# The second FFN product of a one-core diffusion step by Strassen's algorithm

## The chip, the cores and the metric

The kernel runs on one core of a Trainium2 chip. A core has five engines with an instruction queue each: TensorE (matrix products, PE in the profile; its weight loads are PEld), VectorE (DVE), ScalarE (ACT), GpSimd (POOL) and SyncE (SP). SP only issues DMA transfers here, and a few stand on POOL. Results of matrix products go to PSUM; everything else lies in SBUF or in DRAM. The metric is the device time of one execution in microseconds (us).

## The reference, cut to what matters

One layer takes 1024 latent and 128 context tokens of 1024 features through a normalisation, a mixer (recurrence and Fourier branch) and an FFN, with shared weights. The part that the change touches is the FFN and the last normalisation:

```python
    h2 = rmsnorm(x, norm2_g) * (1.0 + scale2) + shift2
    uv = h2 @ ffn_w_in                     # first FFN product:  1024 x 5632
    u = uv[..., :D_FF]
    v = uv[..., D_FF:]                     # D_FF = 2816
    x = x + gate2 * ((jax.nn.silu(u) * v) @ ffn_w_out)   # second FFN product: 2816 x 1024
    ...
y_prompt = rmsnorm(xp, final_g)            # final normalisation, context tokens
y_sample = rmsnorm(xs, final_g)            # and latent tokens
```

All of it is float32.

## The kernel before

**Layout.** Features lie on the 128 partitions and the 1152 tokens (T) along the free axis: x is 8 tiles of 128x1152, and the hidden features silu(u)\*v are 22 tiles (NJ) of 128x1152. A float32 product is made in three passes: each operand is split into a high half (a rounding cast to fp32r by ScalarE) and a low half (the operand minus the high half, by VectorE), and high x high, high x low and low x high are added up in PSUM.

**First FFN product.** It is done by Strassen's algorithm already. A unit j (22 of them) pairs the 128 features j of u with the same ones of v, and the tokens are two halves of 576 (H). The seven products P1, P6, P2, P7, P5, P4, P3 of a unit take 24 matmuls of 128x288 each (`mm_half`, L943), so 168 in a unit; the weights of a product are 512 columns, cast by L1149 and subtracted by L1150 on VectorE, after the weight sums L1161 to L1168. Behind each product VectorE adds its result in (`e6`, `e7`, `e5`, `e4`, `e3`; L1218 to L1239). `e4` and `e3` end with the multiplication by silu(u), and POOL writes the two halves of the hidden tile j to DRAM (`s_d`, L1235 and L1243). The products P1 and P2 of the units 0 to 5 run ahead, beside the second normalisation.

**Second FFN product, as it was.** It is a plain product. `GRPS` cuts the 22 hidden tiles into a group of two and five of four. For a group, `fo_step` goes through the 8 feature blocks m: 3 passes of 3 chunks of 384 tokens for each hidden tile (`mm3`, L241), all in one PSUM tile; `post` adds it, times gate2, to the residual x2[m] on VectorE (L913, L921). The residual's tiles are fetched from DRAM in the first group (L1300). Beside a group the hidden tiles of the next one are fetched (`s_load`, L1261) and split (`s_split`, L245 and L246). The last group runs by token spans instead (`last_step`, L1333: tokens 640 to 1151, 0 to 383, 384 to 639) and adds up the squares of x2 for the final normalisation, partly on POOL. `stat_sum` turns those sums into factors (TensorE sums over the partitions, L260, ScalarE's square root, VectorE's reciprocal), `final_bcast` spreads the factors over the partitions with TensorE (L280, from diagonals of L279), and `final_out` (L1356) makes the outputs.

**What sets the order.** The kernel is scheduled by hand: the instructions of an engine run in the order in which the program emits them. The program is a list of steps; for each the main loop calls `before`, then `advance` (loads of weights on SP some pieces ahead, casts and low halves of the next pieces), then `pe` (the matmuls), `post` and `after`. What is emitted in a step's `post` therefore stands behind the weight splits for the steps ahead. `woven` is a list of tasks that go between the matmuls of a step. Tiles come from pools of fixed size, and an instruction that takes a buffer waits until its last reader is through: 33 buffers of 128x1152 for most operands (`TT`), 4 for short-lived ones such as the fetched hidden tiles `sld` (`LL`), and weight pools that are opened anew by `scope_w`: in the first product 4 raw tiles and 5 split ones, in the second 3 raw tiles of 1024 columns and 3 split ones. In PSUM `G` tiles hold 2 chunks of 288, `Z` tiles 3 chunks of 384.

**The handover.** The last unit's products do more than the others: after the matmuls of P2, `last_p2` fetches and splits the two hidden tiles of the first group, and after those of P3, `last_p3` opens the second product's weight pools and issues the first weight loads.

## Time and profile before

| | |
|---|---|
| Time, median of 3 runs | 1692.13 us (1679.47 to 1692.36) |
| Time of the profiled execution | 1690.14 us |
| Its span | 1688.3 us |
| Mean granted clock of TensorE | 0.994 |
| TensorE busy | 1643.7 us (97% of the span), 10680 matmuls |
| VectorE busy | 1027.6 us (61%) |
| ScalarE busy | 598.0 us (35%) |
| GpSimd busy | 113.8 us (7%) |
| First FFN product, unit by unit | up to 1394.3 us |
| Second FFN product | 1394.5 to 1677.1 us |
| Final normalisation behind it | 1677.1 to 1688.3 us |

Times in the trace count from the start of the span. A row of a timeline has the start, the duration in us, engine, line, operation and tiles (result <- operands); what stands in brackets is the idle time of the engine ahead of it and what ended it. "x10" behind shapes is the number of instructions in a row that the line stands for. Names are the program's, without buffer numbers: g and z are PSUM tiles, w the unit's work tiles, ho and hl split weights, wr raw weights. SPq is SP's DMA queue.

### The profile page before, as it was taken

Reading aid. Unit: us, or ns where it says so; the run is one execution under the profiler, and the core shown is the slowest. Engines: PE = TensorE matmul, PEld = TensorE weight load, DVE = VectorE, ACT = ScalarE, POOL = GpSimd, SP = SyncE. Lnnn points to the kernel's source line nnn. Section 1 sums busy time; section 2 is a strip of 40 time slices with the busy share of each in tenths; the row PEclk is TensorE's granted clock in tenths of the full one; section 3 lists DMA queues with packets and bytes.
Section 4 is the critical chain, followed back from the end, with each engine's and each line's share of the span. In section 5 each row is a group of like instructions: output and inputs, shape, how many; then the busy total and the mean of one; then the engine's idle time right before and its main releaser. Section 6 shows DMA issues by size and latency. Waiting matters only on the chain.

```text
span 1688.3 us, 25378 instructions
## 1 busy us (share of the span) xinstructions
PE 1643.7 (97%) x10680; PEld 1612.8 (96%) x10680; DVE 1027.6 (61%) x1454; ACT 598.0 (35%) x777; POOL 113.8 (7%) x153
## 2 busy tenths in 40 slices
PE   6899999999999999999999999999999999999997
PEld 3799999999999998899999899999999999999997
DVE  6678976777877235734368765555555556444446
ACT  6583127474664223412156322222222232111112
POOL 0200002010101000000000000000000000000012
PEclk9999999999999999999999999999999999999999
DMA  9028832222223035521533232222122236222203
GB/s 376 15 89 311 278 112 98 80 80 92 77 83 129 28 116 192 208 97 61 175 104 121 75 109 87 79 74 70 67 79 72 72 122 245 83 104 80 98 10 113
DMA packets 54177, 192.44 MB, mean 114 GB/s; under 512 B 6384, under 2 KB 8832, under 8 KB 54064
## 3 DMA queue, kind: packets, MB, share of 16 engines
q1 hardware_dynamic: 44624, 154.24, 26.7%
q0 software_dynamic: 9440, 36.58, 5.7%
q8 instruction: 84, 1.38, 0.3%
q14 instruction: 29, 0.24, 0.0%
HBM read 149.45 MB, written 41.30 MB: 113 GB/s over the span
## 4 chain that ended last, share of the span: by engine, by line
PE 77%; DVE 4%; issue 3%; ACT 1%; DMA 0%; POOL 0%; DVEq 0%; SPq 0%; ACTq 0%; POOLq 0%
PE z L241 35%; PE g L943 33%; PE z L1333 3%; PE g L818 1%; PE z L613 1%; PE z L614 1%; PE z L612 1%; PE a L686 1%; PE a L652 0%; DVE ho L1150 0%; DVE hl L207 0%; DVE plo L246 0%; POOL sq L536 0%; DMA sld<-s_d 0%; PE bc L280 0%
## 5 line engine op out<-in xcount | busy, mean ns | idle before, releaser
L241 PE MATMUL z<-hhi,hl 128*128 128x384 f32 x1344 | 280.8, 340 | 0.0
L241 PEld LDWEIGHTS z<-hhi,hl 128*128 128x128 f32 x1344 | 237.8, 188 | 0.8 <-issue 0.8
L943 PE MATMUL g<-b,ho 128*128 128x288 f32 x1584 | 218.9, 296 | 2.2 <-DVE ho L1150 1.2
L943 PEld LDWEIGHTS g<-b,ho 128*128 128x128 f32 x1584 | 213.8, 189 | 2.6 <-DVE ho L1150 1.5
L241 PE MATMUL z<-shi,hl 128*128 128x384 f32 x864 | 175.7, 338 | 0.6 <-DVE x L916 0.6
L206 ACT CAST hl<-wr 128x1024 fp32r<-128x1024 f32 x86 | 89.4, 1042 | 189.4 <-PE z L241 169.6
L241 PEld LDWEIGHTS z<-shi,hl 128*128 128x128 f32 x864 | 153.4, 188 | 1.2 <-issue 0.6
L241 PE MATMUL z<-hlo,hl 128*128 128x384 f32 x672 | 154.5, 338 | 0.0
L943 PE MATMUL g<-t,ho 128*128 128x288 f32 x1056 | 149.5, 297 | 2.8 <-DVE t L1089 2.8
L207 DVE TENSOR_TENSOR hl<-wr,hl 128x1024 fp32r<-128x1024 f32 x86 | 104.6, 1221 | 76.8 <-ACT hl L206 76.0
L943 PEld LDWEIGHTS g<-t,ho 128*128 128x128 f32 x1056 | 144.2, 190 | 3.2 <-DVE t L1089 3.1
L943 PE MATMUL g<-thi,ho 128*128 128x288 f32 x704 | 126.2, 296 | 0.0
L241 PEld LDWEIGHTS z<-hlo,hl 128*128 128x128 f32 x672 | 120.9, 188 | 0.0
L1149 ACT CAST ho<-wr 128x512 fp32r<-128x512 f32 x110 | 64.8, 618 | 155.3 <-DVE wr L1163 139.0
L1150 DVE TENSOR_TENSOR ho<-wr,ho 128x512 fp32r<-128x512 f32 x110 | 75.4, 687 | 60.8 <-ACT ho L1149 60.7
L921 DVE SCALAR_TENSOR_TENSOR x<-z,mods,x 128x768 f32<-128x768 f32 x40 | 40.7, 1017 | 112.6 <-PE z L241 112.6
L943 PEld LDWEIGHTS g<-thi,ho 128*128 128x128 f32 x704 | 104.7, 189 | 0.0
L943 PE MATMUL g<-mx,hl 128*128 128x288 f32 x768 | 102.1, 294 | 0.0
L943 PEld LDWEIGHTS g<-mx,hl 128*128 128x128 f32 x768 | 101.6, 188 | 0.0
L241 PE MATMUL z<-slo,hl 128*128 128x384 f32 x432 | 99.2, 338 | 0.0
L420 DVE SCALAR_TENSOR_TENSOR junk<-adar,cb 128x1024 f32<-128x1024 f32 x64 | 78.3, 1224 | 4.8 <-DMA adar<-in_ada_dram 2.9
L241 PE MATMUL z<-xchi,hl 128*128 128x384 f32 x384 | 79.5, 338 | 0.6 <-ACT sg L391 0.6
(258 smaller groups left out, 2643.4 us busy)
## 6 DMA issues: line engine op xcount, KB each, us to landing
wr<-in_w_uv_dram SPq DMA_DIRECT2D x50, 512.0 KB, 3.6
wr<-in_w_in_dram SPq DMA_DIRECT2D x32, 512.0 KB, 4.2
adar<-in_ada_dram SPq DMA_DIRECT2D x32, 512.0 KB, 5.6
s_d<-w POOLq DMA_DIRECT2D x44, 288.0 KB, 2.4
sld<-s_d SPq DMA_DIRECT2D x22, 576.0 KB, 4.7
wr<-in_w_ff_dram SPq DMA_DIRECT2D x22, 512.0 KB, 3.7
ada<-in_ada_dram SPq DMA_DIRECT2D x16, 512.0 KB, 10.5
wr<-in_w_out_dram SPq DMA_DIRECT2D x13, 512.0 KB, 4.2
```

The costliest lines, as they stand in the source:

```text
L206: nc_a.copy(h[:, 0], r)
L207: nc_v.tensor_sub(h[:, 1], r, h[:, 0].bitcast(F32))
L241: nc_t.matmul(ps[:, c, :CH], w, xx[:, c * CH:(c + 1) * CH], start=(k == first and i == 0), stop=(k == last and i == 2))
L420: nc_v.scalar_tensor_tensor(env["j"], w, 1.0, env["c"][v], op0=ALU.mult, op1=ALU.mult, accum_out=out[:, v:v + 1])
L612: nc_t.matmul(ps, th, rh, start=(k == 0), stop=False)
L613: nc_t.matmul(ps, th, rl, start=False, stop=False)
L614: nc_t.matmul(ps, tl, rh, start=False, stop=(k == KD - 1))
L921: nc_v.scalar_tensor_tensor(dst[:, :768].rearrange("p (c n) -> p c n", c=2), ps[:, 0:2, :CH], mods[:, gq, 0, m:m + 1], src[:, :768].rearra ...
L943: nc_t.matmul(ps[:, c, :HC], w(e, k), xx[:, c * HC:(c + 1) * HC], start=(first and i == 0 and j == 0), stop=(last and i == len(ks) - 1 and ...
L1149: nc_a.copy(h[:, 0], src)
L1150: low = lambda: nc_v.tensor_sub(h[:, 1], src, h[:, 0].bitcast(F32))
L1333: nc_t.matmul(ps[:, b, :hi - lo], ww, xx[:, lo:hi], start=(j == js[0] and i == 0), stop=(j == js[-1] and i == 2))
```

## The change

The second product is now done by Strassen's algorithm too. The 22 hidden tiles are taken as 11 pairs (even tile 2q and odd tile 2q+1), the 8 feature blocks as 4 pairs, the tokens as two halves of 576. B11 and B21 are the first half's tokens of the even and the odd tiles, B12 and B22 the second half's. Operand sums: T1 = B12 - B11, T3 = B22 - B12, T2 = B22 - T1, T4 = B21 - T2. The four weight sums are made in the same manner from the four quarters of the weights.

- `e4` writes a unit's first half to DRAM as B11 or B21. `e3` of an even unit makes T1 and writes it; `e3` of an odd unit writes B22 and makes and writes T3, T2 and T4. B12 isn't written. DRAM holds seven operands (`op_d`) of 11 blocks of 576 tokens in place of `s_d`.
- `ws_tasks` makes the weight sums in 11 parts, one in each of the units 8 to 18: `load` (after P1: four loads of 512 columns on SP), `sums` (after P4: five VectorE operations of 512 columns, and four writes by POOL to `ws_d`).
- The second product takes the products in the order P1, P6, P2, P7, P5, P4, P3 and for each the four feature pairs (`f_steps`). A step pair has 11 blocks, 3 passes and 2 chunks of 288 with `mm_half` in a G tile, the weights being one load of 1408 columns (`fr`), split in two parts of 768 and 640 columns (`f_items`). `f_post` adds the seven results in and updates x2; the sums of squares are on VectorE alone. `after` fetches and splits the next product's operand during the current one, two blocks at a time.
- At the handover `last_p2` fetches and splits the first three parts of B11, and `last_p4` the other three.
- P3 comes last. The final normalisation of the first token half runs woven into it (`fin_sum`, `fin_bcast`, `fin_out`); the last feature pair (`f_last`) goes through its first 288 tokens for all 11 blocks and then through the other 288, and the tail has 3 token tiles left.

The diff's core:

```diff
...
-GRPS = [[0, 1]] + [list(range(s, s + 4)) for s in range(2, NJ, 4)]
+NK = NJ // 2
+WB = NK * P
...
+        open_pool("w", *[[("wraw0", 3), ("whl0", 3)], [("wraw1", 4), ("who1", 5)], [("fraw2", 3), ("fop2", 3)]][n])
...
-    s_d = dr.tile([NJ, P, T], F32, name="s_d")
+    op_d = dr.tile([7, P, NK * H], F32, name="op_d")
+    ws_d = dr.tile([4, P, 4 * WB], F32, name="ws_d")
...
             nc_v.tensor_mul(un.w1[:, H:T], un.w1[:, H:T], un.w2[:, 0:H])
-            nc_p.dma_start(s_d[j][:, 0:H], un.w1[:, H:T])
+            nc_p.dma_start(op_dram("B21" if j % 2 else "B11", j // 2), un.w1[:, H:T])
...
             nc_v.tensor_mul(un.w2[:, H:T], un.w2[:, H:T], un.w1[:, 0:H])
-            nc_p.dma_start(s_d[j][:, H:T], un.w2[:, H:T])
+
+            s1_, s2_, q = un.w1[:, H:T], un.w2[:, H:T], j // 2
+            if j % 2 == 0:
+                nc_v.tensor_sub(un.w1[:, 0:H], s2_, s1_)
+                nc_p.dma_start(op_dram("T1", q), un.w1[:, 0:H])
+                even["w"] = (un.w1, un.w2)
+            else:
+                v1, v2 = even.pop("w")
+                nc_p.dma_start(op_dram("B22", q), s2_)
+                nc_v.tensor_sub(v2[:, 0:H], s2_, v2[:, H:T])
+                nc_p.dma_start(op_dram("T3", q), v2[:, 0:H])
+                nc_v.tensor_sub(v2[:, H:T], s2_, v1[:, 0:H])
+                nc_p.dma_start(op_dram("T2", q), v2[:, H:T])
+                nc_v.tensor_sub(un.w1[:, 0:H], s1_, v2[:, H:T])
+                nc_p.dma_start(op_dram("T4", q), un.w1[:, 0:H])
...
+        def load():
+            box["t"] = []
+            for a in (((0, 0), (1, 0)), ((1, 1), (0, 1))):
+                t = TT("ws", shape=(P, 2, 512))
+                for i, (r, q) in enumerate(a):
+                    nc_s.dma_start(t[:, i], w_ff[r, q][:, o])
+                box["t"].append(t)
+
+        def sums():
+            t, u = box.pop("t")
+            nc_v.tensor_add(u[:, 0], u[:, 0], t[:, 1])
+            nc_v.tensor_add(u[:, 1], u[:, 1], t[:, 0])
+            nc_v.tensor_sub(t[:, 1], t[:, 0], t[:, 1])
+            nc_v.tensor_sub(t[:, 0], u[:, 0], t[:, 0])
+            nc_v.tensor_sub(u[:, 1], u[:, 1], u[:, 0])
+            for i, q in enumerate((u[:, 0], t[:, 0], t[:, 1], u[:, 1])):
+                nc_p.dma_start(ws_d[i][:, o], q)
...
+    def op_load(name, g):
         t = LL("sld")
...
+        n = 2 if g < NK // 2 else 1
+        nc_s.dma_start(t[:, :n * H], op_dram(name, 2 * g, n))
...
+    FSEQ = (("P1", (0, 0), "B11"), ("P6", 1, "T2"), ("P2", (0, 1), "B21"), ("P7", 2, "T3"), ("P5", 0, "T1"),
+            ("P4", (1, 1), "T4"), ("P3", 3, "B22"))
...
+        def dma():
+            r = box["r"] = pools["fraw"].tile([P, WB], F32, name="fr", tag="fr")
+            a = w_ff[src[0], src[1]] if isinstance(src, tuple) else ws_d[src]
+            nc_s.dma_start(r[:], a[:, fp * WB:(fp + 1) * WB])
+
+        def prep(k0, k1):
+            h = pools["fop"].tile([P, 2, KA * P], F32R, name="fo", tag="fo")
+            n, q = (k1 - k0) * P, box["r"][:, k0 * P:k1 * P]
+            nc_a.copy(h[:, 0, :n], q)
+            nc_v.tensor_sub(h[:, 1, :n], q, h[:, 0, :n].bitcast(F32))
...
+    def f_post(name, fp, ps):
...
+        if name == "P1":
+            nc_a.copy(two(v0), z)
+        elif name == "P6":
+            nc_v.tensor_add(two(v1), z, two(v0))
...
+        elif name == "P4":
+            nc_v.tensor_add(two(v0), z, two(v0))
+            add_x(m2, 0, v0)
+            del VV[fp]
+            for m in (m1, m2):
+                acc_sq(m, 0, H)
...
+        def after(h):
+            if pi == 0:
+                x2[h] = TT(f"x2_{h}")
+                nc_s.dma_start(x2[h][:], x2_d[h])
...
+            if 1 <= h <= 4:
+                op_split(nxt, h - 1)
+            if h < 6:
+                op_load(nxt, h)
...
+            for c in range(2):
+                for k in range(NK):
+                    if c == 1 and k == 7:
+                        fin_sum(CH1[0])
+                    if c == 1 and k == 10:
+                        fin_bcast(CH1[0])
...
-                for q in GRPS[0]:
-                    s_load(q)
-                    s_split(q)
+                for g in range(3):
+                    op_load("B11", g)
+                    op_split("B11", g)
...
+                for g in range(3, 6):
+                    op_load("B11", g)
+                    op_split("B11", g)
...
+    for j in range(8, 8 + NK):
+        load, sums = ws_tasks(j - 8)
+        us = unit_last[j]
+        us["P1"].after, us["P4"].after = load, sums
...
+                if fp == 0:
+                    steps[-2].before = lambda: woven.extend([[], [], [], [], [lambda: fin_sum(HALF0)], []])
+                    steps[-1].before = lambda: woven.extend([[], [lambda: fin_bcast(HALF0)], [], [], []])
...
+    c0, c1 = CH1
+    fin_out(c0, [(0, 1), (2, 3)])
+    fin_sum(c1)
+    fin_out(c0, [(4, 5)])
+    fin_bcast(c1)
+    fin_out(c0, [(6, 7)])
+    fin_out(c1, [(0, 1), (2, 3), (4, 5), (6,), (7,)])
```

Where instructions stand now, at three places.

VectorE in one of the units 8 to 18 of the first product, behind its fifth product; w are the work tiles of units, ws the raw tiles of weight sums, ho split weights, g PSUM. Before:

```order
L1232 TENSOR_TENSOR w_11399<-g,w_11311 128x576
L1234 TENSOR_TENSOR w_11311<-w_11311,w_11399 128x576
L1150 TENSOR_TENSOR ho<-wr,ho 128x512
L1239 TENSOR_TENSOR w_11311<-g,w_11311 128x576
L1242 TENSOR_TENSOR w_11399<-w_11399,w_11311 128x576
L1150 TENSOR_TENSOR ho<-sx,ho 128x512 x2
L1218 TENSOR_TENSOR w_11527<-g,w_11527 128x576
```

And now, from the weight sums on, which stand behind the two operations of `e4`:

```order
L1295 TENSOR_TENSOR ws<-ws 128x512
L1296 TENSOR_TENSOR ws<-ws 128x512
L1297 TENSOR_TENSOR ws<-ws 128x512
L1298 TENSOR_TENSOR ws<-ws 128x512
L1299 TENSOR_TENSOR ws<-ws 128x512
L1156 TENSOR_TENSOR ho<-wr,ho 128x512
L1245 TENSOR_TENSOR w_11504<-g,w_11504 128x576
L1248 TENSOR_TENSOR w_11598<-w_11598,w_11504 128x576
L1258 TENSOR_TENSOR w_11366<-w_11598,w_11366 128x576
L1260 TENSOR_TENSOR w_11366<-w_11598,w_11272 128x576
L1262 TENSOR_TENSOR w_11504<-w_11504,w_11366 128x576
L1156 TENSOR_TENSOR ho<-sx,ho 128x512 x2
```

Five weight sums stand between `e4` and the next low half of weights, and in an odd unit three operand sums between `e3` and the two after it (in an even unit one).

SP at the handover; wr and fr are raw weights, sld fetched operands, x_0 to x_7 the residual. Before:

```order
L1145 DMA wr<-in_w_uv_dram 128x1024
L1261 DMA sld<-s_d 128x1152 x2
L1300 DMA x_0_12326<-x_d 128x1152
L195 DMA wr<-in_w_ff_dram 128x1024 x2
L1300 DMA x_1_12371<-x_d 128x1152
L195 DMA wr<-in_w_ff_dram 128x1024 x3
L1261 DMA sld<-s_d 128x1152
```

And now:

```order
L1151 DMA wr<-in_w_uv_dram 128x1024
L1311 DMA sld<-op_d 128x1152 x5
L1311 DMA sld<-op_d 128x576
L1338 DMA fr<-in_w_ff_dram 128x1408 x3
L1436 DMA x_0_12680<-x_d 128x1152
L1311 DMA sld<-op_d 128x1152
L1436 DMA x_1_12719<-x_d 128x1152
```

Six operand loads stand ahead of the second product's first weights, where two and a load of the residual stood before; the weights' loads have 1408 columns instead of 1024.

VectorE from the last sum of squares on; x_0 to x_7 are the residual, yt the outputs, bc the spread factors, dg the diagonals. Before:

```order
L934 TENSOR_TENSOR acc_14112<-acc_14112,sq_14534 128x256
L1356 SCALAR_TENSOR_TENSOR yt<-x_4_12467,vec,bc 128x384
L1356 SCALAR_TENSOR_TENSOR yt<-x_5_12495,vec,bc 128x384
L267 RECIPROCAL rr<-r 128x4
L279 TENSOR_SCALAR dg<-ident,rr 128x128 x2
L1356 SCALAR_TENSOR_TENSOR yt<-x_6_12526,vec,bc 128x384
L1356 SCALAR_TENSOR_TENSOR yt<-x_7_12554,vec,bc 128x384
```

And now:

```order
L1376 TENSOR_TENSOR acc_14460<-acc_14460,sq_15140 128x288
L1477 SCALAR_TENSOR_TENSOR yt<-x_0_12680,vec,bc 128x288
L1477 SCALAR_TENSOR_TENSOR yt<-x_1_12719,vec,bc 128x288
L1477 SCALAR_TENSOR_TENSOR yt<-x_2_12769,vec,bc 128x288
L1477 SCALAR_TENSOR_TENSOR yt<-x_3_12812,vec,bc 128x288
L269 RECIPROCAL rr<-r 128x6
L1477 SCALAR_TENSOR_TENSOR yt<-x_4_12862,vec,bc 128x288
L1477 SCALAR_TENSOR_TENSOR yt<-x_5_12905,vec,bc 128x288
L281 TENSOR_SCALAR dg<-ident,rr 128x128 x2
L1477 SCALAR_TENSOR_TENSOR yt<-x_6_12951,vec,bc 128x288
L1477 SCALAR_TENSOR_TENSOR yt<-x_7_12992,vec,bc 128x288
```

Four outputs of the 288 tokens before the last stand ahead of the reciprocal, two ahead of the diagonals and two behind them; eight outputs of the last 288 tokens follow, as eight of 256 tokens did before.

## Rows read from the trace of the kernel before

**Rows 1.** The page: engines' busy time (share of the span, instructions), the chain's shares, weight loads.

```profile
PE 1643.7 (97%) x10680; PEld 1612.8 (96%) x10680; DVE 1027.6 (61%) x1454; ACT 598.0 (35%) x777; POOL 113.8 (7%) x153
...
PE 77%; DVE 4%; issue 3%; ACT 1%; DMA 0%; POOL 0%; DVEq 0%; SPq 0%; ACTq 0%; POOLq 0%
...
wr<-in_w_uv_dram SPq DMA_DIRECT2D x50, 512.0 KB, 3.6
```

**Rows 2.** Busy by stretch: us, PE, PEld, DVE, ACT, POOL (instructions), clock, DMA share, GB/s.

```profile
941.00:1000.00 59.00, 56.12 (x407) 55.64 (x407) 42.28 (x64) 14.75 (x25) 3.24 (x6) 0.97 0.32 102
1000.00:1100.00 100.00, 100.00 (x752) 100.00 (x751) 58.12 (x86) 23.00 (x41) 5.39 (x10) 1.00 0.25 83
1394.30:1420.00 25.70, 25.13 (x143) 24.45 (x142) 20.25 (x29) 8.16 (x8) 0.54 (x1) 1.00 0.93 357
1623.00:1677.20 54.20, 54.06 (x318) 49.62 (x316) 29.18 (x58) 16.31 (x29) 17.93 (x18) 1.00 0.12 42
1677.20:1688.30 11.10, 1.77 (x8) 1.45 (x8) 7.60 (x19) 1.07 (x3) 0.36 (x1) 0.64 0.66 224
```

**Rows 3.** The chain that ended last, in order of time: start, us, what.

```profile
853.02 1.26 PE bc L280 x10
...
895.65 1.01 PE st L260 x10
...
949.85 444.80 PE g L943 x3322
...
1408.09 215.17 PE z L241 x1224
...
1673.52 0.67 PE bc L280 x6
```

**Rows 4.** Timeline of VectorE, 1140 to 1165 us.

```profile
1141.87 0.76 DVE L1228 TENSOR_TENSOR w<-g,w 128x576 f32<-128x576 f32 x1 [1.84 <-PE g L943]
1142.55 0.68 DVE L1161 TENSOR_TENSOR sx<-wr 128x512 f32<-128x512 f32 x1
...
1164.27 0.76 DVE L1228 TENSOR_TENSOR w<-g,w 128x576 f32<-128x576 f32 x1 [1.84 <-PE g L943]
```

**Rows 5.** DMA of 1394 to 1420 us: totals; issues with KB each and median us to landing.

```profile
DMA packets 2313, 9.17 MB, mean 353 GB/s; under 512 B 269, under 2 KB 269, under 8 KB 2311
...
sld<-s_d SPq DMA_DIRECT2D x5, 576.0 KB, 8.6
```

**Rows 6.** The tile s_d: from its writes' issue to landing.

```profile
DMA to landing us min/median/max: 2.4/2.4/8.8
```

**Rows 7.** Timeline of SP and TensorE, 1380 to 1412 us.

```profile
1384.63 0.81 SPq L195 DMA_DIRECT2D wr<-in_w_ff_dram  x2
...
1394.47 0.68 PE L241 MATMUL z<-shi,hl 128*128 128x384 f32 x3
```

**Rows 8.** Stretches of 1 us, columns as in rows 2.

```profile
950.00:951.00 1.00, 1.00 (x5) 1.00 (x6) 0.41 (x1) 1.00 (x3) 0.00 (x0) 0.50 0.00 0
...
952.00:953.00 1.00, 1.00 (x6) 1.00 (x5) 0.23 (x1) 0.00 (x0) 0.00 (x0) 0.50 0.00 0
```

**Rows 9.** Timeline of TensorE, 944.9 to 957 us.

```profile
949.85 2.88 PE L943 MATMUL g<-t,ho 128*128 128x288 f32 x10 [2.83 <-DVE t L1089]
```

**Rows 10.** Timeline of all engines, 1672 to 1689 us.

```profile
1680.76 4.49 DVE L1356 SCALAR_TENSOR_TENSOR yt<-x,vec,bc 128x384 f32<-128x384 f32 x10
1680.79 1.20 PE L280 MATMUL bc<-dg,ones 128*128 128x128 f32 x4 [0.98 <-DVE dg L279]
```

**Rows 11.** Groups by line and form, 1394 to 1689 us: busy us, mean ns, idle before.

```profile
L246 DVE TENSOR_TENSOR slo<-sld,shi 128x1152 fp32r<-128x1152 f32 x20 | 27.0, 1349 | 3.1 <-ACT shi L245 3.1
L207 DVE TENSOR_TENSOR hl<-wr,hl 128x1024 fp32r<-128x1024 f32 x21 | 25.5, 1219 | 0.2 <-ACT hl L206 0.2
L206 ACT CAST hl<-wr 128x1024 fp32r<-128x1024 f32 x20 | 20.9, 1051 | 169.6 <-PE z L241 169.6
L1356 DVE SCALAR_TENSOR_TENSOR yt<-x,vec,bc 128x384 f32<-128x384 f32 x8 | 4.4, 608 | 0.0
```

More of the change, by code (lines that the diff above doesn't have):

```diff
@@ L934, in accum_sq, with mm_half @@
             add(acc2["a"][:, lo:hi], acc2["a"][:, lo:hi], s)
-    def mm_half(ps, w, ks, xs, first=True, last=True):
+    def mm_half(ps, w, ks, xs, first=True, last=True, again=None):
         for i, k in enumerate(ks):
@@ L943, in mm_half @@
                     nc_t.matmul(ps[:, c, :HC], w(e, k), xx[:, c * HC:(c + 1) * HC],
-                                start=(first and i == 0 and j == 0), stop=(last and i == len(ks) - 1 and j == 2), skip_group_check=not first)
+                                start=(first and i == 0 and j == 0), stop=(last and i == len(ks) - 1 and j == 2), skip_group_check=not first if again is None else again)
     def two(ap):
@@ L1115, in x_of, with op_dram @@
         return f
-    shi, slo = {}, {}
-    fbox = {}
+    OPS = ("B11", "B21", "B22", "T1", "T2", "T3", "T4")
+    def op_dram(name, k0, n=1):
+        return op_d[OPS.index(name)][:, k0 * H:(k0 + n) * H]
+    even = {}
     class Unit:
@@ L1344, in final_bcast, with ws_tasks @@
-    def final_bcast(si):
-        lo, hi = SPANS[si]
-        a = A("bc")
-        nb["bc"] = a
-        stat_bcast(nb["rr"], [a[:, t * P:(t + 1) * P] for t in range((hi - lo) // P)])
-    def final_out(si, groups=((0,), (1,), (2,), (3,), (4,), (5,), (6,), (7,)), bc=None):
-        lo, hi = SPANS[si]
-        bc = nb["bc"] if bc is None else bc
+    def ws_tasks(c):
+        box = {}
+        o = slice(512 * c, 512 * c + 512)
+        def load():
[14 more added lines that the diff above has]
+                nc_p.dma_start(ws_d[i][:, o], q)
+            cost["D"] += 3.4
+        return load, sums
@@ new lines, with op_split @@
+    opset = {n: [None] * NK for n in OPS}
+    raw_op = {}
+    def op_load(name, g):
+        t = LL("sld")
+        n = 2 if g < NK // 2 else 1
+        nc_s.dma_start(t[:, :n * H], op_dram(name, 2 * g, n))
+        raw_op[name, g] = t
+    def op_split(name, g):
+        t = raw_op.pop((name, g))
+        if g < NK // 2:
+            hi, lo = TT("shi", F32R, (P, 2, H)), TT("slo", F32R, (P, 2, H))
+            split(two(t[:, :T]), hi, lo[:], nc_a.copy)
+            for i in range(2):
+                opset[name][2 * g + i] = (hi[:, i], lo[:, i])
+        else:
+            b = TT("shl", F32R, (P, 2, H))
+            split(t[:, :H], b[:, 0], b[:, 1], nc_a.copy)
+            opset[name][2 * g] = (b[:, 0], b[:, 1])
@@ new lines, in add_x, with add_ps @@
+    def add_x(m, half, src):
+        if half == 0:
+            parts = ((0, 0, H),)
+        else:
+            parts = ((0, 0, LAT - H), (1, LAT - H, H))
+        for v, a, b in parts:
+            o = x2[m][:, half * H + a:half * H + b]
+            nc_v.scalar_tensor_tensor(o, src[:, a:b], mods[:, 3, v, m:m + 1], o, op0=ALU.mult, op1=ALU.add)
+    def add_ps(m, ps, c):
+        e = LAT - H - HC
+        for v, a, b in ((0, 0, HC),) if c == 0 else ((0, 0, e), (1, e, HC)):
+            o = x2[m][:, H + c * HC + a:H + c * HC + b]
+            nc_v.scalar_tensor_tensor(o, ps[:, c, a:b], mods[:, 3, v, m:m + 1], o, op0=ALU.mult, op1=ALU.add)
@@ L1353, in final_out, with fin_out @@
+    def fin_out(spans, groups):
+        lo, hi = spans[0][0], spans[-1][1]
         for ks in groups:
@@ L1456 @@
         steps.append(st)
+    unit_last = {}
     for j in range(NJ):
```

223 lines of the change are left out of this document (118 added, 105 removed).

## The prediction

> **What bounds the kernel now.** First the page's busy times and its chain [rows 1]: TensorE is busy for 97% of the span, and 77% of the chain that ended last is its matmuls. So the kernel is a row of TensorE stages, and what a change in one stage is worth is read there. Next, busy time by stretch [rows 2]: from 1000 us on, in the first FFN product, TensorE has no idle time, while VectorE is busy 58.12 of 100 us; the second product, 1394.30 to 1677.2 us, is as full except for about half a microsecond at its start. After 1677.2 us the last normalisation is left, where TensorE does 1.77 of 11.10 us. So a matmul less in the second product is time gained, as long as VectorE, ScalarE and the loads keep up.
>
> The reference time is the second product and what follows it: from its first matmul at 1394.47 us [rows 7] to the end of the span at 1688.3 us, 293.8 us.
>
> **Matmuls.** Before, the second product is 1584 chunk products (22 row blocks, 8 feature blocks, 3 passes, 3 chunks), in 128x384 form at 215.17/1224 = 175.8 ns each [rows 3]. After, it is 7 products of 4 feature pairs of 11 block pairs in 3 passes and 2 chunks, 1848 matmuls of 128x288. That form is the first product's own: there the same VectorE instruction of two units in a row starts at 1141.87 and 1164.27 us [rows 4], and between them lie 168 matmuls, so 22.40/168 = 133.3 ns. 1848 x 133.3 ns = **246.4 us**. Bounds: by columns alone (175.8/384 ns) 243.7 us; by 444.80/3322 ns of the first product's piece of the chain [rows 3] 247.4 us.
>
> **The handover.** Before, SP has two operand loads and one of the residual ahead of the first weights, which are issued at 1384.63 us, 10 us before they are needed [rows 7]. After, six loads stand ahead of the first weights on SP, and they share four buffers: the fourth to the sixth wait until VectorE has split the second, third and fourth. That fourth split stands behind the sum that reads P5 of the last unit, and P5 ends two products (6.4 us) before the first product does. From P5's end: the sum 0.76 [rows 4], the split 1.35 [rows 11], so the sixth load and the weights behind it leave at 2.2. The weights are 704 KB. A 512 KB load lands 3.6 us after issue in the first product [rows 1]; 192 KB more and the 288 KB ahead cost 0.5 and 0.8 us at the 353 GB/s of this stretch [rows 5]. They land at 7.1, ScalarE's cast of 768 columns (from 1051 ns for 1024, [rows 11]) takes 0.8, and TensorE can start at 7.9 instead of 6.4. VectorE's low half comes 0.95 later (from 1219 ns for 1024), of which four matmuls (0.53) cover a part: 0.4 more. The other five blocks' weights stand behind the last unit's sums and come about 0.4 late. Together **2.3 us**. Below: 0, if the loads overlap better. Above: if each landing in the series (third, fourth, sixth load) takes the 8.6 us seen in this stretch [rows 5] instead of 4.9 as just worked out, some 12 us. VectorE's last sums and ScalarE's casts queue behind those splits too, and TensorE waits for both.
>
> A gap has a second price. TensorE once stood still for 2.83 us up to 949.85 us [rows 9], and then ran at a granted clock of 0.50, the 1.2 GHz level, from 950 to 953 us [rows 8]: its next ten matmuls took 2.88 instead of 1.33 us. The Trainium skill, "TensorE: Matmul & The Clock Gate", section "HAM oscillation", says the same in general: gaps between bursts put the clock back to half and the next burst starts slow; the trace agrees. [...] I expect one of 1.5 us, half of that at 949 us, and add nothing; the upper bound holds it.
>
> **Normalisation sums inside the stream.** Five token tiles of the first half (sums 1.01, broadcast 1.26 us) and three of the next quarter (broadcast 0.67, sums about as much) on TensorE [rows 3]: **3.5 us**. The first half's factors are asked for three weight blocks after its last update: VectorE needs an add, an update and two square sums of 0.76, which leaves TensorE waiting about 0.3, and about 1.2 us more for the square root's table and the diagonals behind a weight split. **1.5 us**; bounds 0 and 4.
>
> **The tail.** Before, 11.2 us from the last matmul: an update, a square, a sum, then outputs; VectorE ends its ten last ones at 1685.25, 3.05 us before the end [rows 10]. After: two updates, square and sum 1.55; four outputs of 288 columns before the reciprocal at 0.45 (between 0.42 for 256 and 0.55 for 384 columns, from 4.49 us for eight and two [rows 10]), 1.8; reciprocal 0.2, two outputs 0.9, diagonals 0.25 to the first broadcast; 3 broadcasts of two passes at half clock 1.8 (before, 2 took 1.20); eight outputs 3.6; 3.05. **13.2 us**; bounds 12.8 and 15.4 (0.61 per output by the mean of [rows 11]).
>
> **Costed at nothing.** In units 8 to 18 of the first product VectorE gets five weight sums (0.68 each like L1161), and of all 22 every even unit one operand sum, every odd one three (0.76 like L1228, [rows 4]): 55 x 0.68 + 44 x 0.76 = 71 us. Its idle time covers them: 42 of every 100 us [rows 2]. Followed through an odd unit, the sums end 10 us after P4; the next weights whose low half waits behind them are due 2 to 3 us later, and the sums that free PSUM for P4 and P3 of the next unit are on time. Without cover they would cost their 71 us. Bound: in 941 to 1000 us, with VectorE busy 42.28 of 59, TensorE lost 2.9 us [rows 2]; I keep 5 us above, 0 below.
>
> POOL issues 121 writes instead of 44. They landed after 2.4 us, at most 8.8 [rows 6]; a weight sum's buffers are needed again 8 us or more later. The Trainium skill, "SBUF — State Buffer", section "SBUF: two separate sides", warns that POOL's DMAs can be held up by VectorE instructions that take the port they share with it, copies above all. The median of 2.4 us at VectorE's 58% speaks against it here, and the added instructions have two tensor inputs. By that rule, landings of 8.8 us in units 8 to 18 would bring the next unit's weights, which stand on SP behind those buffers, 2 us late, or 22 us in all.
>
> Within the second product VectorE gets 28 weight splits (1.75), 7 operand sets (5 x 1.35 + 0.75) and some 55 us of updates, sums and outputs, about 157 of 250 us; ScalarE less. Per product 35 us of matmuls stand against 6.0 MB, 171 GB/s. The first also fetches the residual, 4.7 MB, and starts the next: 12.6 MB, 36 us at 353 GB/s. That nearly fills it, but its last transfers are due only in the next product.
>
> **Sum.** 2.3 + 246.4 + 3.5 + 1.5 + 13.2 = 266.9 against 293.8 us: 26.9 us less. The profiled execution's own time is 1690.14 us (span 1688.3), so 1663.2 us; the median of the runs shown, 1692.13, is 2 us above it. I take **1664 us**, 1.7% less.
>
> **Rivals.**
> - The handover stalls 12 us, as bounded above. For it: the series of waits and the slow landings. Against: the third load leaves early. 1673 us. Chance 0.06.
> - The loads bound the first of the seven products. If they ran at 245 GB/s, 12.6 MB would take 51 us against 35; 8 us of it are needed only later. 1672 us. Against: 353 GB/s here. Chance 0.05.
> - VectorE's burst in the first product makes TensorE wait in each of units 8 to 18. At 1.5 us per unit it takes back 16.5 us: 1680 us, within 1%. Chance 0.09. At 2.4 us the whole gain is gone; at 4.5 us it is 49.5 us lost: 1713 us, **slower**. For it: 947 to 950 us, where TensorE waited 2.83 us for such a difference [rows 9]. Against: in that stretch VectorE is busy 72% on the whole with longer chains before TensorE, here 58% and (5 x 0.68 + 2 x 0.76)/22.4, 80%, with 2 us to spare in each unit. Chance 0.05.
> - The change doesn't save: if a matmul cost the same whatever its width, 1848 x 175.8 ns = 324.9 us, 1742 us. The 133.3 ns speak against it. Chance 0.01.
>
> **Numbers.** The forecast, with 1656 to 1672 us as its own range, has 0.74. The low end takes a handover without a gap, matmuls by columns, and the spread of the runs of before (lowest 1679.47); the high end takes the first two rivals and their bounds: 1652 to 1678 us. About 1% is what a measurement of this kernel can tell from no change. Faster by over 1% is below 1675: the forecast and the first two rivals, 0.84; within 1% 0.10; slower 0.06.
>
> **What would show it.** Right: a first product that ends at 1394 us as before, without TensorE idle time in units 8 to 18; a gap of 1 to 3 us at the handover, with the first weights behind six operand loads; 1848 matmuls in about 246 us; a tail near 13 us. Wrong: TensorE waiting for VectorE in the first product, for loads in the first of the seven products, or a low granted clock at the handover.

## The result, and the profile after

The changed kernel takes **1666.87 us** (median of four runs, 1665.14 to 1668.87), the kernel before 1692.24 us beside it. The ratio is 0.9859, with a 95% interval of 0.983 to 0.9889: 1.4% faster, 25.4 us by the medians. A second comparison on another chip gave 1669.01 us and 0.9847 (0.9822 to 0.9871). The forecast was 1664 us, the range 1652 to 1678 us.

The profiled execution of the changed kernel took 1667.6 us, its span is 1665.8 us. Its engines and its chain, as in [rows 1]:

```profile
PE 1616.8 (97%) x10952; PEld 1588.3 (95%) x10952; DVE 1098.4 (66%) x1535; ACT 635.1 (38%) x829; POOL 137.3 (8%) x213
...
PE 74%; DVE 6%; issue 3%; ACT 2%; DMA 1%; POOL 0%; DVEq 0%; SPq 0%; ACTq 0%; POOLq 0%
```

VectorE has 70.8 us more to do and TensorE 26.9 us less than in [rows 1]. Busy time by stretch (columns as in [rows 2]: us; busy us and instructions of PE, PEld, DVE, ACT, POOL; granted clock; DMA share; GB/s):

```profile
1000.00:1100.00 100.00, 99.82 (x749) 99.61 (x748) 65.12 (x96) 24.57 (x43) 10.25 (x19) 1.00 0.37 127
1100.00:1200.00 100.00, 100.00 (x752) 100.00 (x751) 74.94 (x114) 24.38 (x44) 18.75 (x35) 1.00 0.51 177
...
1614.00:1652.60 38.60, 36.79 (x275) 35.73 (x273) 23.13 (x50) 11.81 (x20) 0.00 (x0) 1.00 0.17 62
1652.60:1665.80 13.20, 2.26 (x12) 2.10 (x12) 8.45 (x22) 1.11 (x3) 0.00 (x0) 0.60 0.53 179
```

From 1100 to 1200 us all the sums are being made: VectorE is busy 74.94 us (54.79 us in the same stretch before), and TensorE still has no idle time. The chain that ended last (start, us, what):

```profile
1019.43 361.83 PE g L945 x2712
...
1386.47 5.00 DMA sld<-op_d
...
1393.31 4.40 DMA fr<-in_w_ff_dram
...
1404.98 206.14 PE fp L945 x1544
```

The second product runs at 206.14/1544 = 133.5 ns a matmul. Between the two products the chain leaves TensorE: it goes over an operand load and the first weights' load. TensorE's timeline there, and SP's:

```profile
1393.88 3.36 PE L945 MATMUL g<-b,ho 128*128 128x288 f32 x24
1398.69 0.53 PE L945 MATMUL fp<-shi,fo 128*128 128x288 f32 x2 [1.45 <-ACT fo L1343]
...
1399.69 0.80 PE L945 MATMUL fp<-shi,fo 128*128 128x288 f32 x4 [0.20 <-DVE fo L1344]
...
1404.98 0.79 PE L945 MATMUL fp<-shi,fo 128*128 128x288 f32 x4 [0.24 <-DVE fo L1344]
```

```profile
1380.00 13.26 SPq L1311 DMA_DIRECT2D sld<-op_d  x4
1393.31 1.38 SPq L1338 DMA_DIRECT2D fr<-in_w_ff_dram  x3
```

The last product of 24 matmuls starts at 1393.88 and would end at 1397.08 us (24 x 133.3 ns); the second product starts at 1398.69, so 1.6 us are lost, and 0.44 us more in two small waits. The first weights left at 1393.31 us, behind four operand loads that took SP 13.26 us. At the end (timeline of PE and DVE):

```profile
1619.22 1.53 PE L282 MATMUL bc<-dg,ones 128*128 128x128 f32 x10 [1.08 <-DVE dg L281]
...
1646.60 0.40 PE L1498 MATMUL fp<-shi,fo 128*128 128x288 f32 x1 [0.61 <-DVE x L1365]
...
1651.92 0.64 PE L1498 MATMUL fp<-shl,fo 128*128 128x288 f32 x3
...
1657.23 1.46 PE L282 MATMUL bc<-dg,ones 128*128 128x128 f32 x6 [2.01 <-DVE dg L281]
1658.73 3.49 DVE L1477 SCALAR_TENSOR_TENSOR yt<-x,vec,bc 128x288 f32<-128x288 f32 x8 [0.60 <-PE bc L282]
```

The last matmul ends at 1651.92 + 0.64 = 1652.56 us, 13.24 us ahead of the end.

Against the trace of before: from the end of the first product to the end of the span it was 293.8 us and is 1665.8 - 1397.08 = 268.7 us, 25.1 us less. The whole span is only 22.5 us shorter, since the first product ended 2.6 us later than before (1397.08 against 1394.47 us [rows 7]). Of that 1.6 us lie ahead of the first product's units already, where nothing was changed: the matmuls behind the wait of 2.83 us that [rows 9] shows at 949.85 us start at 951.42 us now, and between 947.79 and 952.66 us in the traces of the experiments below, so this is a difference between executions. New waits of 0.37 us stand behind the units 1 and 3 (timeline of TensorE); the other 0.7 us are not traced to a row.

```profile
951.42 2.88 PE L945 MATMUL g<-t,ho 128*128 128x288 f32 x10 [2.83 <-DVE t L1091]
...
987.02 3.43 PE L945 MATMUL g<-b,ho 128*128 128x288 f32 x24 [0.19 <-DVE w L1234]
...
1019.43 3.42 PE L945 MATMUL g<-b,ho 128*128 128x288 f32 x24 [0.18 <-DVE w L1234]
```

### The profile page after: what moved, and what is told of

The parts are those of the page before. It is cut to its first block, busy times and chain, and to the rows that moved or that the text cites. A ratio compares the mean times of both kernels' runs of the same rounds, so it can differ in the third digit from the quotient of the medians.

```text
span 1665.8 us, 26346 instructions
## 1 busy us (share of the span) xinstructions
PE 1616.8 (97%) x10952; PEld 1588.3 (95%) x10952; DVE 1098.4 (66%) x1535; ACT 635.1 (38%) x829; POOL 137.3 (8%) x213
## 3 DMA queue, kind: packets, MB, share of 16 engines
q1 hardware_dynamic: 54640, 184.16, 32.3%
## 4 chain that ended last, share of the span: by engine, by line
PE 74%; DVE 6%; issue 3%; ACT 2%; DMA 1%; POOL 0%; DVEq 0%; SPq 0%; ACTq 0%; POOLq 0%
PE g L945 31%; PE z L243 23%; PE fp L945 14%; PE z L615 1%; PE z L616 1%; PE z L614 1%; PE g L820 1%; DVE ho L1156 1%; PE fp L1498 1%; PE a L688 1%; PE a L654 0%; DVE yt L1477 0%; DVE plo L248 0%; DVE hl L209 0%; POOL sq L538 0%
## 5 line engine op out<-in xcount | busy, mean ns | idle before, releaser
L945 PE MATMUL fp<-shi,fo 128*128 128x288 f32 x1080 | 193.3, 296 | 1.9 <-ACT fo L1343 1.4
L945 PEld LDWEIGHTS fp<-shi,fo 128*128 128x128 f32 x1080 | 160.2, 189 | 2.6 <-ACT fo L1343 1.7
L209 DVE TENSOR_TENSOR hl<-wr,hl 128x1024 fp32r<-128x1024 f32 x65 | 79.1, 1222 | 78.1 <-ACT hl L208 77.3
L945 PE MATMUL fp<-slo,fo 128*128 128x288 f32 x540 | 116.0, 296 | 0.0
L945 PEld LDWEIGHTS fp<-slo,fo 128*128 128x128 f32 x540 | 86.9, 189 | 0.0
L1343 ACT CAST fo<-fr 128x768 fp32r<-128x768 f32 (+1 forms) x56 | 43.6, 781 | 109.1 <-PE fp L945 107.7
```

The source lines that it names most:

```text
L209: nc_v.tensor_sub(h[:, 1], r, h[:, 0].bitcast(F32))
L945: nc_t.matmul(ps[:, c, :HC], w(e, k), xx[:, c * HC:(c + 1) * HC], start=(first and i == 0 and j == 0), stop=(last and i == len(ks) - 1 and ...
L1343: nc_a.copy(h[:, 0, :n], q)
```

## The experiments

Two of the forecast's steps were worth testing. One is that VectorE's sums cost nothing because there are 2 us to spare in each unit: the trace shows no wait, but doesn't show how near one is. The other is what makes the gap at the handover. Where the text says "in one run", there is no interval, and the reading rests on the trace.

**Handover: the four buffers.** Only the buffers of the last three operand loads are changed.

```diff
-    def op_load(name, g):
-        t = LL("sld")
+    def op_load(name, g, new=None):
+        t = (new or LL)("sld")
...
                 for g in range(3, 6):
-                    op_load("B11", g)
+                    op_load("B11", g, TT)
```

> The last three operand loads of the handover take buffers of the large pool instead of the four short-lived ones, so they no longer wait for VectorE's splits; nothing else is changed. In the changed kernel the sixth of these loads was issued at 1392.94 us, the first weights at 1393.31 us, and TensorE stood still for 1.45 us in front of the second product and for 0.20 and 0.24 us within its first 7 us. If the series of four buffers sets the gap (my theory), the weights leave about 5 us earlier, the 1.45 us go and the time falls by 1.5 to 2 us, to about 1665 us. If the weight pools' opening or the bandwidth sets it (the loads of this stretch then only crowd each other), the weights still land after 1397 us and the gap stays at 1.2 us or more, the time at about 1667 us.

Measured: 1664.4 us, ratio 0.9823 (0.9794 to 0.9852). Timeline of SP and TensorE:

```profile
1387.02 1.29 SPq L1338 DMA_DIRECT2D fr<-in_w_ff_dram  x3
...
1392.40 3.36 PE L945 MATMUL g<-b,ho 128*128 128x288 f32 x24
1395.60 0.43 PE L945 MATMUL fp<-shi,fo 128*128 128x288 f32 x2
```

The weights leave 5.4 us ahead of the last product instead of 0.6 us, and the second product starts 3.20 us after the last product's start, with no gap; of the small waits of 0.20 and 0.24 us, 0.13 us in all is left. The 2.5 us between the medians are not clear of noise (the intervals of the two ratios overlap), and in the profiled executions 1.6 of the 4.1 us between the spans lie ahead of the first product; it is the missing gap in the trace that decides. So the series of loads that waited for each other's buffers made the gap, and neither the pools' opening nor the bandwidth.

**More VectorE work behind `e4`.** Pairs of a sum and its inverse ahead of the five weight sums, two pairs in the first run, five in the second.

```diff
             t, u = box.pop("t")
+            for _ in range(2):
+                nc_v.tensor_add(u[:, 0], u[:, 0], t[:, 1])
+                nc_v.tensor_sub(u[:, 0], u[:, 0], t[:, 1])
```

> Each of the eleven parts of the weight sums has four VectorE operations of 512 columns more (a sum and its inverse, twice, in place), 2.7 us a unit, 30 us in all; the result of the sums stays the same. The prediction gave each unit 2 us to spare behind its sums. By that TensorE waits about 0.7 us in each of the units 8 to 18, some 8 us in all: about 1675 us. If VectorE's idle time as a whole is the cover (it was busy for about 74 of 100 us in these units, so 5.8 us of 22.4 are left), nothing is lost: 1667 us. If the queue behind the sums has no room at all, the 30 us show in full: 1697 us.

> As the run with four more operations, but with ten more in each part, 6.8 us a unit, 75 us in all. By 2 us to spare in a unit, 4.8 us x 11 = 53 us are lost: about 1720 us. By the idle time as a whole (5.8 us in a unit of 22.4) 1 us x 11 = 11 us are lost: about 1678 us. If each unit recovers later and TensorE's queue of ready weights hides more than that, less than 5 us.

Measured: 1700.61 us (ratio 1.0047, 1.0028 to 1.0065) with four operations more, and 1762.07 us in one run with ten: 33.7 and 95.2 us above the changed kernel's median, for 30 and 75 us of added work. All of the gain is gone with the first. In the first run neither the 2 us of room nor the idle time as a whole held; the third theory's number came close, though its reason, no room at all, was not quite it. In the second run all three theories were far too low. The timelines of ScalarE and TensorE show what is late, of the changed kernel first and then of the one with four more:

```profile
1109.78 0.69 ACT L1247 ACTIVATE w<-w 128x576 f32<-128x576 f32 x1 [6.10 <-DVE w L1245]
...
1110.88 0.63 ACT L1215 COPY w<-g 128x576 f32<-128x576 f32 x1
...
1112.29 3.36 PE L945 MATMUL g<-b,ho 128*128 128x288 f32 x24
```

```profile
1113.97 0.68 ACT L1247 ACTIVATE w<-w 128x576 f32<-128x576 f32 x1 [9.01 <-DVE w L1245]
...
1115.07 0.63 ACT L1215 COPY w<-g 128x576 f32<-128x576 f32 x1
...
1115.75 3.46 PE L945 MATMUL g<-b,ho 128*128 128x288 f32 x24 [2.02 <-ACT w L1215]
...
1140.43 4.97 PE L945 MATMUL g<-b,ho 128*128 128x288 f32 x24 [2.02 <-ACT w L1215]
```

TensorE's P2 of the next unit waits for `e1`, ScalarE's copy of P1's result (L1215). That copy stands on ScalarE behind the silu of the last unit's `e3` (L1247) and a cast, the silu waits for VectorE's sum (L1245), and that sum stands behind the weight sums. In the changed kernel the copy ends at 1111.51 us and P2 starts at 1112.29: 0.78 us to spare. Four operations more let ScalarE wait 9.01 instead of 6.10 us for VectorE, 2.9 us longer (0.73 each), so about 2.9 - 0.78 = 2.1 us should be waited; it is 2.02 us, in each of the eleven units. In four of the eleven the clock fell besides (4.97 us instead of 3.46 for the 24 matmuls): 11 x 2.02 + 4 x 1.5 + some 0.26 us a unit of slower starts is 31 us; the second product started 32.3 us later. With ten more the wait is 6.37 us (by 7.3 - 0.78: 6.5) and the clock fell every time:

```profile
1150.56 5.56 PE L945 MATMUL g<-b,ho 128*128 128x288 f32 x24 [6.38 <-ACT w L1215]
```

**More VectorE work in the units 1 to 5.**

```diff
+            for _ in range(5 if 0 < j < 6 else 0):
+                nc_v.tensor_add(un.w1[:, 0:512], s1_[:, 0:512], s2_[:, 0:512])
```

> Five VectorE operations of 512 columns, as many as the weight sums of a unit, are added in each of the units 1 to 5 (ahead of the operand sums, into a work tile that is overwritten), 3.4 us a unit, 17 us in all; the result stays the same. In these units five products of 3.2 us run instead of seven. In the changed kernel TensorE waited 0.19 and 0.18 us behind the units 1 and 3, whose operand sums are three. If these units have no room left (my theory), each of the five waits 3 us or more: 15 to 17 us in all, about 1683 us. If the units' place doesn't matter and VectorE has room there as it has later, the loss is under 3 us.

Measured: 1680.89 us in one run, 14 us more; the second product starts 13.3 us later, 1.0 us of it from ahead of these units. TensorE waited six times for VectorE behind these units, 9.85 us together, and lost 1.5 us to the clock once:

```profile
987.83 4.93 PE L945 MATMUL g<-t,ho 128*128 128x288 f32 x24 [2.78 <-DVE w L1230]
...
1006.88 3.42 PE L945 MATMUL g<-t,ho 128*128 128x288 f32 x24 [1.32 <-DVE w L1230]
```

So the units of five products have little room; but no wait reached the 3 us that were expected, and of 17 us some 5 were still absorbed.

**The same work in another place, first try.** Four of nine operations behind the sum after P6, the part's loads half a unit earlier.

```diff
...
+        def more():
+            t, u = box["t"]
+            for _ in range(2):
+                nc_v.tensor_add(u[:, 0], u[:, 0], t[:, 1])
+                nc_v.tensor_sub(u[:, 0], u[:, 0], t[:, 1])
...
-        us["P1"].after, us["P4"].after = load, sums
+        unit_last[j - 1]["P5"].after = load
+        us["P4"].after, us["P6"].after = sums, more
```

> The same nine VectorE operations in each part of the weight sums as in the run that cost 33.7 us, but four of them stand behind the sum after P6 of the unit instead of ahead of the five (the part's loads are issued half a unit earlier for that). In the run with all nine behind e4, TensorE waited 2.02 us at P2 of each next unit for ScalarE's copy of P1's result; that copy stands behind the last unit's silu, which waits for VectorE's sum in e3, which stands behind the nine. In the changed kernel the copy ended at 1111.51 us and P2 began at 1112.29: 0.78 us to spare. If the place in front of this chain sets the loss (my theory now), the four operations fall into VectorE's idle time behind P6 (1.76 and 1.31 us there) and nothing is lost: 1665 to 1669 us. If the amount of VectorE work sets it, the loss stays near 30 us: about 1697 us.

Measured: 1678.33 us, ratio 0.9926 (0.9907 to 0.9944): 11.5 us above the changed kernel, neither theory's number. TensorE's waits in front of P2 are six (8.1 us), and they have another cause, as ScalarE's group by line (busy, mean ns, idle before and what ended it) and its timeline show:

```profile
L1215 ACT COPY w<-g 128x576 f32<-128x576 f32 x14 | 9.0, 640 | 17.9 <-DMA ws_d<-ws 13.1 <-PE g L945 3.6 <-issue 1.1
```

```profile
1132.46 0.60 ACT L1155 CAST ho<-sx 128x512 fp32r<-128x512 f32 x1
1135.22 0.64 ACT L1215 COPY w<-g 128x576 f32<-128x576 f32 x1 [2.16 <-DMA ws_d<-ws]
```

The copy now waits for a buffer: the earlier loads hold two buffers longer, so the copy's work tile is one that a weight sum is still being written out from. The six waits, one fall of the clock (4.98 us for the 24 matmuls behind the wait of 2.07 us) and slower starts make about 11 of the 11.5 us. The run left the question open.

**The same work in another place, second try.** The four operations behind P6 work on the unit's own tile, and no load is moved.

```diff
+        def more(un=unit_of[j]):
+            w, b = un.w1[:, 0:512], b22[0][:, 0, 0:512].bitcast(F32)
+            for _ in range(2):
+                nc_v.tensor_add(w, w, b)
+                nc_v.tensor_sub(w, w, b)
+        us["P6"].after = more
```

> Four VectorE operations of 512 columns are added behind the sum after P6 in each of the units 8 to 18, on the unit's own work tile (a tile of the normalised activations is added and taken away again, twice); everything else is as in the changed kernel, loads and buffers too. So VectorE does nine operations more than before the change per unit here, as in the two runs that lost 33.7 and 11.5 us against it, but holds no buffer longer. In the second of those the waits that were left (0.38 to 2.07 us in front of P2) came from ScalarE's copy of P1's result, which waited for a work buffer that a write of the weight sums to DRAM had not yet left. If place in the queue and buffers are all that sets the loss (my theory), TensorE waits nowhere in the units 8 to 18: 1665 to 1669 us. If the amount of VectorE work has a share of its own, about 10 us or more remain: 1677 us or above.

Measured: 1666.37 us, ratio 0.9843 (0.9828 to 0.9857), the time of the changed kernel (1669.01 us and 0.9847 on the same chip). Busy time over the units 8 to 18, of the changed kernel and of this one:

```profile
1090.00:1345.00 255.00, 255.00 (x1915) 255.00 (x1914) 185.07 (x280) 63.81 (x113) 43.41 (x81) 1.00 0.52 181
```

```profile
1090.00:1345.00 255.00, 254.61 (x1917) 254.31 (x1916) 213.59 (x324) 64.22 (x113) 43.60 (x81) 1.00 0.53 180
```

VectorE is busy 84% of the time instead of 73%, with the same count of nine operations as in the run that lost 33.7 us, and TensorE waits 0.39 us in all. So it was not the amount of VectorE work, but its place in front of ScalarE's chain that made the loss.

**Loads: eight copies more.**

```diff
+    cp_d = dr.tile([KD, P, T], F32, name="cp_d")
...
                 nc_s.dma_start(x2[h][:], x2_d[h])
+                nc_s.dma_start(cp_d[h], p_d[h])
```

> Beside each of the eight residual loads in the first of the seven products, a copy of 576 KB from DRAM to DRAM, 4.7 MB in all, is issued on SP; its result is not used. In the changed kernel the DMA engines were full from 1395 to 1430 us (380 to 420 GB/s) and TensorE did not wait. If 8 us of the transfers are needed only later (the prediction's count), the 11 to 12 us that 4.7 MB take at 400 GB/s cost 3 to 4 us: about 1671 us. If this stretch was just at its bound, they show in full, 11 to 12 us: about 1678 us. If the loads are far from a bound, nothing.

Measured: 1670.23 us in one run, 3.4 us more, the number of the first theory but not for its reason. Once the first of the seven products runs, TensorE waits for no transfer; it lost its time at the start, with a wait of 2.02 instead of 1.45 us, and then to the clock (granted 0.83 in the mean from 1400 to 1410 us):

```profile
1400.25 0.53 PE L946 MATMUL fp<-shi,fo 128*128 128x288 f32 x2 [2.02 <-ACT fo L1344]
1401.24 1.33 PE L946 MATMUL fp<-shi,fo 128*128 128x288 f32 x4 [0.20 <-DVE fo L1345]
```

```profile
1400.00:1410.00 10.00, 9.55 (x58) 9.32 (x59) 7.09 (x9) 2.96 (x5) 3.23 (x6) 0.83 1.05 409
```

4.7 MB more, nearly 12 us of transfers, were absorbed behind it. Whether the copies or the spread of executions made the handover 0.57 us longer stays open, as it is one run.

**Loads: the residual ahead of the weights.**

```diff
-            if pi == 0:
+            if pi == 0 and x2[h] is None:
...
                 scope_w(2)
+                for h in range(6):
+                    x2[h] = TT(f"x2_{h}")
+                    nc_s.dma_start(x2[h][:], x2_d[h])
                 advance(state["prep"] + 2, state["prep"] + 1)
```

> Six of the eight residual loads (3.5 MB) are issued ahead of the second product's first weights; as nothing else is changed, they share SP's queue with them. The prediction let a handover stall cost 12 us at most, and expected a short gap to leave the clock alone: TensorE's granted clock stayed at full speed after 1.45 us at the handover, fell to half after 2.83 us at 949 us, and after 2.02 us in front of P2 it fell in four units of nine and not in the others. By 400 GB/s the 3.5 MB take 9 us; the buffers that they wait for (those of the first product's operands) add some. So a gap of 9 to 13 us at the handover, behind it a half clock for about 3 us (1.5 us lost): 1676 to 1681 us. If loads of this size overlapped with the weights instead of standing ahead of them, the gap would be under 3 us: about 1668 us.

Measured: 1676.12 us in one run, in the expected range.

```profile
1406.92 0.85 PE L945 MATMUL fp<-shi,fo 128*128 128x288 f32 x2 [11.53 <-ACT fo L1343]
```

```profile
1400.00:1410.00 10.00, 3.08 (x13) 3.07 (x13) 2.35 (x3) 2.27 (x4) 0.00 (x0) 0.51 1.00 408
```

The gap is 11.53 us, and the granted clock behind it is at its lower level (0.51 in the mean of 1400 to 1410 us). That is 10.1 us more than the 1.45 us of the changed kernel, for 3.5 MB that take 8.7 us at this stretch's 408 GB/s. So loads ahead of the first weights cost their full time: the order on SP matters at the handover, and the forecast's stall of 12 us is what six loads in the wrong place make. (The expectation speaks of a clock that fell in four units of nine; the full count is four of eleven.)

**Handover and end.** The large pool's buffers as above; the broadcast two weight blocks later, a PSUM tile for each chunk of the last pair, the first chunk's sums, broadcast and two outputs earlier.

```diff
-            ps = G("fp")
             for c in range(2):
+                ps = G("fp")
                 for k in range(NK):
-                    if c == 1 and k == 7:
+                    if c == 1 and k == 5:
                         fin_sum(CH1[0])
-                    if c == 1 and k == 10:
+                    if c == 1 and k == 9:
                         fin_bcast(CH1[0])
...
+                else:
+                    fin_out(CH1[0], [(0, 1)])
...
-                    steps[-1].before = lambda: woven.extend([[], [lambda: fin_bcast(HALF0)], [], [], []])
+                    steps[-1].before = lambda: woven.extend([[], [], [], [lambda: fin_bcast(HALF0)], []])
...
```

> The handover's last three operand loads in buffers of the large pool (the run of that alone took 1664.4 us, without a gap), and three changes at the end: the broadcast of the first half's factors stands two weight blocks later (TensorE waited 1.08 us for the diagonals there), the last pair's two chunks have a PSUM tile each (0.61 us waited between them), and sums, broadcast and two of the outputs of the first chunk stand earlier, so that VectorE has 14 outputs behind the last matmul instead of 16. If these waits are what the second product's 26.9 us of gain lost on the way, TensorE's waits of 1.08 and 0.61 us go and the tail of 13.24 us shrinks by about 1: 1661 to 1662 us. If TensorE waits for the same work elsewhere, or the tail is set by the last transfer, 1664 us as without them.

Measured: 1661.68 us, ratio 0.9828 (0.9788 to 0.9867); all four runs (1653.15 to 1663.69) lie below the first four of the changed kernel, but the intervals of the two ratios overlap. Its trace:

```profile
1608.72 1.42 PE L282 MATMUL bc<-dg,ones 128*128 128x128 f32 x10
...
1638.44 0.55 PE L1498 MATMUL fp<-shl,fo 128*128 128x288 f32 x3
...
1642.61 5.18 DVE L1477 SCALAR_TENSOR_TENSOR yt<-x,vec,bc 128x288 f32<-128x288 f32 x12
1642.64 0.83 PE L282 MATMUL bc<-dg,ones 128*128 128x128 f32 x6 [1.00 <-ACT dg L279]
```

The waits of 1.08 and 0.61 us are gone, and the end (span 1651.4 us) comes 12.4 us after the last matmul instead of 13.24. Most of this difference is the broadcast: its six matmuls took 0.83 us here, at a granted clock of 1.00, and 1.46 us in the changed kernel, at 0.50.

**Two outputs on other engines.**

```diff
...
+                    nc_a.copy(side, nb["bc", CH1[0]][0][:, :hi - lo])
+                    t = nb["side"] = TT("yt", shape=(P, 2, hi - lo))
+                    for i in range(2):
+                        nc_p.tensor_mul(t[:, i], x2[6 + i][:, lo:hi], side)
...
```

> The handover's buffers and the three changes at the end, as in the run that took 1661.68 us, and besides two of the first chunk's last outputs are made on GpSimd and ScalarE (from a copy of the spread factors in SBUF), so that VectorE has 12 instead of 14 outputs behind the last matmul, at 0.43 to 0.45 us each. If VectorE's outputs set the end, 0.9 us less: 1660.8 us. If the transfer of the outputs sets it, no change against 1661.7 us.

> The changed kernel as it is, on the same chip as the two others, so that they can be compared with it: 1664 to 1669 us as before; the kernel with the better handover and end 5 to 6 us below it.

Measured: 1663.37 us (0.9819, 0.9803 to 0.9835), and 1669.01 us for the changed kernel beside it. No gain over the run before. VectorE had two outputs less, but its last eight waited for the broadcast, which took 1.46 instead of 0.83 us (granted clock 0.50 instead of 1.00), and the end came 13.75 us after the last matmul (1647.85 to 1661.6 us):

```profile
1652.19 1.46 PE L282 MATMUL bc<-dg,ones 128*128 128x128 f32 x6 [0.99 <-ACT dg L279]
1653.69 3.49 DVE L1477 SCALAR_TENSOR_TENSOR yt<-x,vec,bc 128x288 f32<-128x288 f32 x8 [0.60 <-PE bc L282]
```

VectorE is through at 1657.18 us, 9.3 us after the last matmul (8.8 in the run before), and the transfers need 4.4 us more (3.6). So the number is that of the second theory, no change, but not by the transfers alone: the broadcast's clock took back part of what two outputs less gave. That is one profiled execution of each kernel. Both kernels with the better handover and end are 5 to 6 us faster than the changed kernel by the medians; against it the intervals overlap, and one of its four runs beside them took 1661.05 us. Against the kernel before both are clearly faster.

## Why the prediction was right, and where it was not

- **Matmuls** (246.4 us): 1848 x 133.5 ns = 246.7 us. The form's price from the first product held, and with it the whole of the gain.
- **Handover** (2.3 us): 1.6 us and the two small waits of 0.44, 2.05 us. The steps fit too: P5 ended at 1390.68, the weights left at 1393.31, 2.6 us later (2.2 predicted), and landed in 4.40 us (4.9). That four buffers make the series is shown by the run without it. The clock stayed up after this gap, as assumed, but that was luck in part: behind the same gap of 1.45 us in the run with ten more operations a unit it fell (TensorE's timeline, and a stretch of 1 us with the granted clock of 0.50):

```profile
1492.14 0.53 PE L945 MATMUL fp<-shi,fo 128*128 128x288 f32 x2 [1.45 <-ACT fo L1346]
1494.00:1495.00 1.00, 1.00 (x6) 1.00 (x6) 0.50 (x1) 1.00 (x3) 0.00 (x0) 0.50 1.06 359
```

- **Sums in the stream** (3.5 and 1.5 us): the sums took 1.28 and 0.72 us, the broadcasts 1.53 and 0.75, together 4.3 us; the waits were 1.08 and 0.61 us. The second of these was not foreseen: the second chunk of the last pair waited because VectorE was reading the first one in the same PSUM tile. With all terms as measured the sum is 268.0 us; the other 0.7 of the 1.8 us by which the forecast's sum was short (268.7 against 266.9 us) may be slower starts behind each stop, which is not shown.
- **Tail** (13.2 us): 13.24 us, by errors that cancel: the broadcast was 0.3 us shorter than assumed and some smaller terms too, the end after VectorE's last output 3.6 instead of 3.05 us.
- **Costed at nothing**: TensorE's idle time in the units 8 to 18 is zero, so the number was right. Its reason was not, and in that the number was luck. The step that failed is "with 2 us to spare in each unit", which came from the low halves of weights and the sums that free PSUM, both VectorE's own. The chain that ends last goes over ScalarE: sum, silu, a cast, the copy of P1's result. It has 0.78 us to spare. By that, one VectorE operation more in that place (0.73 us) would use up nearly all of the room; from four to ten of them the wait grew from 2.02 to 6.37 us in every unit, 0.73 us for each, and the clock cost more besides. The 0.37 us behind the units 1 and 3, where three operand sums met a unit of five products, were inside the 5 us kept for such waits.
- **Writes by POOL**: they landed after 2.8 us at the median, 9.1 at most for operands, 2.7 and 5.3 us for weight sums, with VectorE busy for 75 of 100 us; before, the operands' writes took 2.4 and 8.8 us [rows 6]. The Trainium skill, "SBUF — State Buffer", section "SBUF: two separate sides", had warned of POOL's transfers behind VectorE; no run here shows such a delay.
- **Rivals**: the loads as a bound fell, since 4.7 MB more made TensorE wait for none of them. A stall of 12 us is what a wrong order on SP gives. The rival of VectorE's burst was nearer than its chance of 0.14 says. (The forecast and the first two rivals add up to 0.85, not 0.84.) Against the forecast's 26.9 us the trace gained 25.1; of the rest 1.0 us is in the sums and waits at the end.

## What to carry to other kernels

When work is hidden in an engine's idle time, its place in that engine's queue decides, not the idle time as a whole: follow every instruction behind it to who waits, over the other engines' queues too, and take the smallest slack. Four operations of the same size in each of eleven units cost 33.7 us ahead of a sum that another engine's chain waits for, and nothing behind the sum after P6. Loads that wait for each other's buffers ahead of a stage's first weights make a gap that a few free buffers take away.

## What was not expected of the hardware

- **The clock after short waits.** One and the same gap can have two prices. At the handover TensorE's granted clock stayed up in five traces with gaps of 1.40 to 1.53 us, but it fell to 0.50 in the run with ten more operations a unit (1.45 us), in the second try of place (1.64 us) and in the run with the copies (2.02 us). After waits of 2.02 us in front of P2 the next 24 matmuls took 4.97 us in four units and some 3.45 us in seven. After 2.83, 6.37 and 11.53 us it was at the lower level each time. The Trainium skill, "TensorE: Matmul & The Clock Gate", section "HAM oscillation — how this bites in real kernels", tells of waits for transfers that set the clock back, with a slow burst behind them. The runs agree for the long gaps; what decides after the short ones no run here shows.
- **A faster stretch in one execution.** The profiled execution of the kernel with the better handover and end did 772 matmuls of 128x288 in 100 us of the first product, others 752, at the same granted clock of 1.00:

```profile
1100.00:1200.00 100.00, 100.00 (x772) 100.00 (x771) 77.05 (x117) 26.52 (x47) 19.30 (x36) 1.00 0.52 183
```

  That is 129.5 instead of 133.0 ns each, from about 1040 us to the end of that product, some 9 us; that execution took 1653.15 us, the three others of the same kernel 1661.36 to 1663.69. What makes it is open; the second product ran at 752 again. Single executions of other kernels were 8 to 13 us faster than their neighbours too (1679.47 us before, 1655.5 us with the four buffers, 1661.05 us of the changed kernel), but no trace of them is kept.
